# Convolution taps and gate columns in the order of the source on VectorE, and the first weight roundings behind the first chunk of h

## The chip, the cores and the metric

One core of a Trainium2 chip runs the kernel. The metric is the device time of one execution in microseconds; the time before is 794.59 us, the median of three runs (794.29 to 795.41). The engines are TensorE (PE, with its weight loads as PEld), VectorE (DVE), ScalarE (ACT), GpSimd (POOL) and SyncE (SP), whose queue issues the DMAs here.

## The reference

One decoder layer on 512 positions of 2048 channels. The part that matters, cut:

```python
c_act = silu(c)
mod = c_act @ w_ada + b_ada                      # 3 x 2048 values: shift, scale, gate
h = x * (1 + scale) + shift
q, k, v, g_attn, glu_a, glu_b, g_conv = split(h @ w_in)
y_attn = banded_sink_attention(q, k, v, rel_bias, sinks) * silu(g_attn)   # window 128, 16 q heads, 4 kv heads
u = glu_a * sigmoid(glu_b)                       # 1024 channels
u = causal_depthwise_conv(u, conv_w) + conv_b    # 31 taps
y_conv = (silu(layer_norm(u)) @ w_pw + b_pw) * silu(g_conv)
y = concat(y_attn, y_conv) @ w_out
x = layer_norm(ALPHA * x + gate * y)
```

## The kernel before

All large products run at about fp32 precision as three passes. Each fp32 operand is rounded to `hi` (fp32r) on ScalarE (L175), and `lo = raw - hi` is taken on another engine (L176, VectorE unless the call names GpSimd). `mm3` then adds hi*hi (L188), hi*lo (L189) and lo*hi (L190) into one PSUM tile. Where the weights are the left operand, L188 and L189 read `wh` and L190 reads `wl`; in the product with `w_out` the weights are on the right, so L189 reads `wl`.

Stage 1 (`ph1`, to about 200 us) builds h in 16 chunks of 128 channels. For each chunk VectorE reduces two 128 x 2048 blocks of `w_ada` with silu(c) (L225), takes `s1 = scale + 1` (L244), ScalarE makes `hh` and `h` from `xT` (L246, L247), and VectorE makes `hl` (L248). At once `fix` and `rot` project the chunks done so far to the 16 column tiles of glu_a and glu_b: `fix` keeps six PSUM tiles open, `rot` sums the other ten through SBUF (`acc`). `plan()` gives the order: h 0, fix 0, rot 3 over chunk 0, rot 4 over chunk 0, h 1, fix 1, rot 5 over two chunks, and so on. `make_u` turns a pair of column tiles into the gated input `u` of the convolution, eight tiles in all.

Stage 2 runs `project` for the column blocks of 256 in the order k, v, then q and g_attn for each of four head groups, then four blocks of g_conv (`gc`). A projection is four weight blocks of 512 KB; a block is `load_w` (raw, rounding, `wl`), then 24 matmuls into two PSUM tiles, with stages of the attention of the head group before (`between`, two per block: scores L440 to L455, transposes L462, values L472 to L484). An attention step of 128 queries takes four of these places, so two blocks. After each block `take(conv, budget)` draws work for VectorE from a generator, until the costs that it yields use up the budget. `wl` is made on GpSimd up to the second gc projection and on VectorE in the last two. Weight tiles (`wr`, `wh`, `wl`) have three buffers each. k is evicted by ScalarE and VectorE in eight pairs of instructions (L397 and L398), q in four (L503 and L504), g_attn and gc by ScalarE alone (L510, L527).

The generator `conv_and_gate` yields taps and gate columns. The convolution takes channel tiles in four pairs, and in a pair the 31 taps alternate between the two tiles, each tap an instruction on 128 x 512 that adds to a sum in PSUM (`cva`, two buffers, L294 and L300); the last tap writes `cv` in SBUF. That is 248 instructions, 240 of which yield 0.6; the opening tap of a tile yields nothing. Behind every second yielded tap comes one half of a gate column: a DMA of 512 KB of `w_ada` (`wag`, one buffer for each half) and a reduction on VectorE (L316), 32 in all at a cost of 1.4. The budgets are 4.0 for k and v, 2.3 for q, g_attn and the first two gc blocks, 4.8 for the last two gc blocks (L69). Then `take(fill, 1000)` (L625) draws what is left, and the first part of the layer norm over channels.

Stage 3 multiplies the attention half of y with `w_out`, a column block of 512 at a time into four PSUM tiles (`quad`): three of the pools `prj` or `att`, and the fourth of `cva`. It also finishes the norm; then come the pointwise product, the second half of `w_out` and the last layer norm.

The order of instructions on each engine is not that of the source. A planner (`schedule_with_timeline_sim=True`, L805) follows the program with its own durations and puts on each engine, when it falls free, the first instruction in the source's order whose inputs and buffers are ready. So a tap, which is almost always ready, can be placed ahead of an instruction that stands earlier in the source but has to wait. On the chip an engine then takes its instructions in the order that was planned.

Of the kernel before, what the change touches and what calls it, by code (L numbers as in the profile page):

```python
# [13 lines left out]
AF = mybir.ActivationFunctionType  # L14
ALU = mybir.AluOpType
# [4 lines left out]
S = 512  # L20
# [27 lines left out]
SM_CB = 48  # L48
# [8 lines left out]
N_FIXED = 3  # L57
# [44 lines left out]
def parts_of(k0, n):  # L102

    m = -(-n // 4)
    cuts = [k0 + n * a // m for a in range(m + 1)]
    return list(zip(cuts[:-1], cuts[1:]))
# [34 lines left out]
def build(tc, xT, x, c, wadaT, smalls, win, wpw, wout, relT, sinks, ln_g, ln_b, out):  # L141
    nc = tc.nc
    es = ExitStack()

    blocks, off = {}, 0
    for key, k0, n, cols in w_in_blocks():
        width = n * sum(w for _, w in cols)
# [11 lines left out]
    sm = pp.tile([P, SM_N], F32, name="sm")  # L159
# [3 lines left out]
    first = pp.tile([P, 1], F32, name="first")  # L163
# [6 lines left out]
    wp = es.enter_context(tc.tile_pool(name="wp", bufs=3, reuse_waits="tile"))  # L170
    cvp = es.enter_context(tc.tile_pool(name="cvp", bufs=10, reuse_waits="tile"))

    def split(raw, hi, lo, engine=None):

        nc.scalar.activation(hi, raw, AF.Copy)  # L175
        (engine or nc.vector).tensor_tensor(lo, raw, hi.bitcast(F32), op=ALU.subtract)  # L176

    def load_w(src, off, width, pool=None, space=1024, engine=None):
        pool = pool or wp
        raw = pool.tile([P, space], F32, name="wr")  # L180
        nc.sync.dma_start(raw[:, :width], src[off:off + P * width].rearrange("(p e) -> p e", p=P))
        hi = pool.tile([P, space], F32R, name="wh")
        lo = pool.tile([P, space], F32R, name="wl")
        split(raw[:, :width], hi[:, :width], lo[:, :width], engine)
        return hi, lo

    def mm3(ps, lh, ll, rh, rl, start, stop):
        nc.tensor.matmul(ps, lh, rh, start=start, stop=False)  # L188
        nc.tensor.matmul(ps, lh, rl, start=False, stop=False)  # L189
        nc.tensor.matmul(ps, ll, rh, start=False, stop=stop)  # L190

    def silu_c(pool, psp, tag):

        warm = psp.tile([P, S], F32, name="warm", tag=tag)
        for i in range(N_WARM):
            nc.tensor.matmul(warm[:, :P], ones, ones, start=True, stop=True)
        crow = pool.tile([P, D], F32, name="wa", bufs=WA_BUFS)[0:1, :]
        nc.sync.dma_start(crow, c)
        cb = pool.tile([P, D], F32, name="cb", bufs=1)
        parts = [slice(i * S, (i + 1) * S) for i in range(4)]  # L200

        chl = [(hh[0:1, NK - 4 + i, :], hl[0:1, NK - 4 + i, :]) for i in range(4)]
        for part, (hi, lo) in zip(parts, chl):
            split(crow[:, part], hi, lo)
        for part, (hi, lo) in zip(parts, chl):
            ps = psp.tile([P, S], F32, name="psc", tag=tag)
            nc.tensor.matmul(ps, ones_r[0:1, :], hi, start=True, stop=False)
            nc.tensor.matmul(ps, ones_r[0:1, :], lo, start=False, stop=True)
            nc.scalar.activation(cb[:, part], ps, AF.Silu)
        warm = psp.tile([P, S], F32, name="warm", tag=tag)  # L210
        for i in range(N_WARM2):
            nc.tensor.matmul(warm[:, :P], ones, cb[:, D - P:], start=True, stop=True)
        return cb
# [15 lines left out]
    glu = {}  # L229
    ph1 = ExitStack()  # L230
    p1 = ph1.enter_context(tc.tile_pool(name="p1", bufs=2))
    ps1 = ph1.enter_context(tc.tile_pool(name="ps1", bufs=2, space=PSUM))
    fixed = [ps1.tile([P, S], F32, name=f"fix{t}", bufs=1) for t in range(2 * N_FIXED)]
    cb = silu_c(p1, ps1, "rot")
# [13 lines left out]
        nc.vector.tensor_tensor(hl[:, k, :], h, hh[:, k, :].bitcast(F32), op=ALU.subtract)  # L248

    def fix(k):  # L250
        wh, wl = load_w(win, *blocks["fix", k], p1, N_FIXED * 256)
        for t in range(2 * N_FIXED):
            cs = slice(t * P, (t + 1) * P)
            mm3(fixed[t], wh[:, cs], wl[:, cs], hh[:, k, :], hl[:, k, :], k == 0, k == NK - 1)
# [6 lines left out]
    def rot(i, k0, n):  # L261
        ps = [ps1.tile([P, S], F32, name="rot") for _ in range(2)]
        for ka, kb in parts_of(k0, n):
            wh, wl = load_w(win, *blocks["rot", i, ka])
            for t in range(2):
                for k in range(ka, kb):
                    o = (k - ka) * 256 + t * P
                    mm3(ps[t], wh[:, o:o + P], wl[:, o:o + P], hh[:, k, :], hl[:, k, :], k == k0, k == k0 + n - 1)
        for t in (0, 1):
            if k0 == 0:  # L270
                nc.scalar.activation(acc[i, t], ps[t], AF.Copy)
            else:
                nc.vector.tensor_tensor(acc[i, t], ps[t], acc[i, t], op=ALU.add)  # L273
        if k0 + n == NK:
            make_u(i, acc[i, 0], acc[i, 1])

    def make_u(i, a, b):
        sig = p1.tile([P, S], F32, name="sig", bufs=1)
        nc.scalar.activation(sig, b, AF.Sigmoid)
        glu[i] = new_u()  # L280
        nc.vector.tensor_tensor(glu[i][:, PAD:], a, sig, op=ALU.mult)
# [3 lines left out]
    def conv_steps():  # L285

        sums = {}
        for i0 in range(0, NC8, 2):
            for j in range(TAPS):
                for i in (i0, i0 + 1):  # L290
                    w = sm[:, SM_CW + i * TAPS + j:SM_CW + i * TAPS + j + 1]
                    if j == 0:
                        sums[i] = ps2.tile([P, S], F32, name="cva", bufs=2)
                        nc.vector.tensor_scalar(sums[i], glu[i][:, :S], w, sm[:, SM_CB + i:SM_CB + i + 1],  # L294
                                                op0=ALU.mult, op1=ALU.add)
                        continue
                    if j == TAPS - 1:
                        cv[i] = cvp.tile([P, PAD + S], F32, name="cv", tag="u")
                    dst = cv[i][:, :S] if j == TAPS - 1 else sums[i]
                    nc.vector.scalar_tensor_tensor(dst, glu[i][:, j:j + S], w, sums[i], op0=ALU.mult, op1=ALU.add)  # L300
                    yield 0.6

    def gate_steps():

        cb = ys.tile([P, D], F32, name="cbg", tag="sgc0")
        nc.sync.dma_start(cb, c.to_broadcast([P, D]))
        nc.scalar.activation(cb, cb, AF.Silu)
        junk = cvp.tile([P, PAD + S], F32, name="junkg", tag="u")[:, :S].bitcast(BF16)
        for j in range(2 * NK, 3 * NK):
            dst = mod[:, j:j + 1]  # L310
            for half in range(2):
                hs = slice(half * S * 2, (half + 1) * S * 2)
                wa = ys.tile([P, 2 * S], F32, name="wag", tag=f"y{2 + half}")
                nc.sync.dma_start(wa, wadaT[j * P:(j + 1) * P, hs])
                first = sm[:, SM_ADA + j:SM_ADA + j + 1]
                nc.vector.tensor_tensor_reduce(junk, wa, cb[:, hs], 1.0, dst if half else first, ALU.mult, ALU.add,  # L316
                                               dst)
                yield 1.4

    def conv_and_gate():  # L320
        gate = gate_steps()
        for n, cost in enumerate(conv_steps()):
            yield cost
            if n % 2:
                yield next(gate, 0)
        yield from gate
# [42 lines left out]
    def project(c0, evac, budget, new_ps, gen=None, after=None, between=lambda: None, engine=nc.gpsimd):  # L369
        ps = [new_ps() for _ in range(2)]  # L370
        for k0 in range(0, NK, 4):
            wh, wl = load_w(win, *blocks["col", c0, k0], engine=engine)
            for t in range(2):
                between()
                for kk in range(4):
                    o = kk * 256 + t * P
                    mm3(ps[t], wh[:, o:o + P], wl[:, o:o + P], hh[:, k0 + kk, :], hl[:, k0 + kk, :],
                        k0 + kk == 0, k0 + kk == NK - 1)
            take(gen or conv, budget)
            if after:  # L380
                after(k0)
        for t in range(2):
            evac(t, ps[t])
# [21 lines left out]
    for k0 in range(0, NK, 4):  # L405
        wh, wl = load_w(win, *blocks["col", C_V, k0], engine=nc.gpsimd)
        for n in range(NB):
            o = vps[n // 2][:, n % 2, :]
            for kk in range(4):
                k = k0 + kk  # L410
# [6 lines left out]
    for n in range(NB):  # L417
        split(vps[n // 2][:, n % 2, :].rearrange("p (j d) -> p j d", j=NKV), vhl[:, n, :, 0, :], vhl[:, n, :, 1, :])
# [209 lines left out]
    def w_out_block(n, kp):  # L628
        return load_w(wout, (n * 8 + kp) * P * 1024, 1024)
# [9 lines left out]
    for n in range(4):  # L639
        cs = slice(n * S, (n + 1) * S)  # L640
        ps = quad(n)
        for kp in range(4):
            wh, wl = w_out_block(n, kp)
# [45 lines left out]
    for o in range(4):  # L689
        ps = [prj() for _ in range(2)]  # L690
        for k0 in range(0, NC8, 4):
            wh, wl = load_w(wpw, (o * 2 + k0 // 4) * P * 1024, 1024)
            for t in range(2):
                for kk in range(4):
                    w0 = kk * 256 + t * P
                    k = k0 + kk
# [3 lines left out]
        for t in range(2):  # L700
            i = 2 * o + t
            yc = small("yc")[:, :S]
            nc.vector.scalar_tensor_tensor(yc, ps[t], sm[:, SM_PB + i:SM_PB + i + 1], sgc[i // 4][:, i % 4, :],
                                           op0=ALU.add, op1=ALU.mult)
# [30 lines left out]
    for n in range(2):  # L735
        ps = quad(n)
        for kp in range(4, 8):
            wh, wl = w_out_block(n, kp)
# [8 lines left out]
    for t in range(NB):  # L747
# [12 lines left out]
        for m in range(4):  # L760
            ms = slice(m * S, (m + 1) * S)
            nc.vector.scalar_tensor_tensor(z[:, t, ms], z[:, t, ms], mv[:, t, 0:1], lg[:, ms],
                                           op0=ALU.subtract, op1=ALU.mult)
        nc.vector.reciprocal(mv[:, t, 3:4], mv[:, t, 2:3])
        for m in range(4):
            ms = slice(m * S, (m + 1) * S)
            nc.vector.scalar_tensor_tensor(z[:, t, ms], z[:, t, ms], mv[:, t, 3:4], lb[:, ms],
                                           op0=ALU.mult, op1=ALU.add)
# [40 lines left out]
```

## Time and profile before

| | |
|---|---|
| median of three runs | 794.59 us |
| profiled execution, device time | 794.61 us |
| span of its instructions | 792.8 us |
| TensorE matmuls, weight loads | 763.5, 629.0 us busy |
| VectorE | 646.4 us busy, 1053 instructions |
| ScalarE, GpSimd | 344.4, 124.9 us busy |
| mean granted clock of TensorE | 0.991 |

The profile is one execution. Times of rows count from the start of the span. Busy time of TensorE overlaps from one matmul to the next, so a busy TensorE may still be at half its clock; the granted clock says which (1.00 is 2.4 GHz, 0.5 is 1.2 GHz). An idle time in brackets stands before the row's first instruction, with what ended it.

### The profile page before, as it was taken

The page shows a single profiled execution, that of the slowest core. Times are in us where ns is not written, and L with a number is a line of the kernel's source. Part 1 is how long each engine was busy: PE and PEld are TensorE (multiplying, and loading weights), DVE is VectorE, ACT ScalarE, POOL GpSimd, SP SyncE. Part 2 cuts the span into 40 slices and gives each one's busy share as a digit, 9 for nine tenths or more (in the row PEclk, how much of TensorE's full clock was granted, in tenths as well). Part 3 has the DMA queues.
Part 4 walks back from the last instruction along what each step waited for, and adds up shares of the span by engine and source line. Part 5 has one row for each costly group of instructions (what it writes and reads, how often), then busy time and mean ns, then how long its engine had stood idle before and what let it go on. Part 6 is the DMA issues. An engine that isn't in the chain of part 4 may idle for free.

```text
span 792.8 us, 9710 instructions
## 1 busy us (share of the span) xinstructions
PE 763.5 (96%) x3522; PEld 629.0 (79%) x3522; DVE 646.4 (82%) x1053; ACT 344.4 (43%) x576; POOL 124.9 (16%) x78
## 2 busy tenths in 40 slices
PE   5999999999999889899999999999999999999994
PEld 4787888878898678688888888888888888888883
DVE  6888988946999999999999999764674219867797
ACT  4543333333342143666585668534475335433000
POOL 0000000002535253243333333000000000000000
PEclk9999999999999999999999999999999999999998
DMA  8999998513777676332222222223223233684033
GB/s 311 414 412 407 346 322 305 191 59 112 243 259 239 230 247 211 108 110 77 91 95 83 79 81 80 81 82 105 87 76 121 88 107 120 226 296 156 0 107 107
DMA packets 39091, 136.11 MB, mean 172 GB/s; under 512 B 4338, under 2 KB 6786, under 8 KB 34818
## 3 DMA queue, kind: packets, MB, share of 16 engines
q1 hardware_dynamic: 39042, 135.49, 48.9%
q8 instruction: 27, 0.44, 0.2%
q14 instruction: 22, 0.17, 0.1%
HBM read 131.26 MB, written 4.22 MB: 171 GB/s over the span
## 4 chain that ended last, share of the span: by engine, by line
PE 79%; DVE 15%; DMA 3%; issue 2%; ACT 1%; SPq 0%; DVEq 0%; ACTq 0%
PE prj L190 13%; PE prj L188 13%; PE prj L189 13%; DVE junkg L316 6%; PE rot L188 5%; DVE cva L300 4%; PE rot L189 4%; PE rot L190 4%; PE fix L188 3%; PE att L190 3%; PE att L189 3%; PE att L188 3%; PE fix L189 3%; PE fix L190 3%; DMA wag<-in_wadaT 2%
## 5 line engine op out<-in xcount | busy, mean ns | idle before, releaser
L175 ACT ACTIVATE wh<-wr 128x1024 fp32r<-128x1024 f32 (+2 forms) x129 | 127.3, 996 | 177.1 <-PE prj L189 68.0
L188 PE MATMUL prj<-hh,wh 128*128 128x512 f32 x480 | 190.5, 397 | 2.6 <-ACT sg L510 2.1
L189 PE MATMUL prj<-hl,wh 128*128 128x512 f32 x480 | 189.1, 394 | 0.0
L190 PE MATMUL prj<-hh,wl 128*128 128x512 f32 x480 | 188.1, 394 | 0.0
L176 POOL TENSOR_TENSOR wl<-wr,wh 128x1024 fp32r<-128x1024 f32 x48 | 120.0, 2503 | 316.4 <-ACT wh L175 297.6
L300 DVE SCALAR_TENSOR_TENSOR cva<-u,sm,cva 128x512 f32<-128x512 f32 x232 | 163.0, 746 | 0.6
L176 DVE TENSOR_TENSOR wl<-wr,wh 128x1024 fp32r<-128x1024 f32 (+3 forms) x81 | 89.0, 1103 | 71.4 <-ACT wh L175 71.2
L188 PEld LDWEIGHTS prj<-hh,wh 128*128 128x128 f32 x480 | 90.9, 189 | 22.9 <-ACT sg L510 2.6
L190 PEld LDWEIGHTS prj<-hh,wl 128*128 128x128 f32 x480 | 90.8, 189 | 18.7
L189 PEld LDWEIGHTS prj<-hl,wh 128*128 128x128 f32 x480 | 91.1, 190 | 18.0
L225 DVE CUSTOM_DVE_ANT_0 junk<-wa,cb,sm 128x2048 bf16<-128x2048 f32 (+1 forms) x32 | 72.9, 2278 | 2.7 <-DMA wa<-in_wadaT 2.7
L188 PE MATMUL rot<-hh,wh 128*128 128x512 f32 x160 | 62.5, 395 | 1.0 <-DVE acc L273 1.0
L189 PE MATMUL rot<-hl,wh 128*128 128x512 f32 x160 | 62.5, 390 | 0.0
L190 PE MATMUL rot<-hh,wl 128*128 128x512 f32 x160 | 62.4, 391 | 0.0
L451 ACT ACTIVATE e<-e,least 128x257 f32<-128x257 f32 (+1 forms) x64 | 30.4, 476 | 37.0 <-DVE least L446 34.4
L189 PE MATMUL fix<-hl,wh 128*128 128x512 f32 x96 | 38.8, 404 | 0.0
L190 PE MATMUL fix<-hh,wl 128*128 128x512 f32 x96 | 38.2, 398 | 0.0
L188 PEld LDWEIGHTS rot<-hh,wh 128*128 128x128 f32 x160 | 30.3, 190 | 8.9 <-DVE acc L273 1.1
L246 ACT ACTIVATE hh<-xt,mod,s 128x512 fp32r<-128x512 f32 x16 | 13.0, 815 | 51.7 <-DVE mod L225 45.3
L190 PEld LDWEIGHTS rot<-hh,wl 128*128 128x128 f32 x160 | 30.0, 188 | 6.8 <-DVE wl L176 0.3
L273 DVE TENSOR_TENSOR acc<-rot,acc 128x512 f32<-128x512 f32 x34 | 23.1, 688 | 14.9 <-PE rot L190 14.9
L189 PEld LDWEIGHTS rot<-hl,wh 128*128 128x128 f32 x160 | 30.0, 188 | 6.4
(186 smaller groups left out, 1307.4 us busy)
## 6 DMA issues: line engine op xcount, KB each, us to landing
wr<-in_win SPq DMA_DIRECT2D x68, 512.0 KB, 3.6
wa<-in_wadaT SPq DMA_DIRECT2D x30, 1024.0 KB, 7.8
wag<-in_wadaT SPq DMA_DIRECT2D x32, 512.0 KB, 4.2
wr<-in_wout SPq DMA_DIRECT2D x32, 512.0 KB, 3.3
wr<-in_win SPq DMA_DIRECT2D x24, 384.0 KB, 8.2
xt<-in_xT SPq DMA_DIRECT2D x16, 256.0 KB, 8.6
wr<-in_wpw SPq DMA_DIRECT2D x8, 512.0 KB, 3.3
xs<-in_x SPq DMA_DIRECT2D x16, 256.0 KB, 5.4
```

What stands on the lines that cost most here:

```text
L175: nc.scalar.activation(hi, raw, AF.Copy)
L176: (engine or nc.vector).tensor_tensor(lo, raw, hi.bitcast(F32), op=ALU.subtract)
L188: nc.tensor.matmul(ps, lh, rh, start=start, stop=False)
L189: nc.tensor.matmul(ps, lh, rl, start=False, stop=False)
L190: nc.tensor.matmul(ps, ll, rh, start=False, stop=stop)
L225: nc.vector.tensor_tensor_reduce(junk[:, part], w[:, part], cb[:, part], 1.0, first, ALU.mult, ALU.add, mod[:, j:j + 1])
L246: nc.scalar.activation(hh[:, k, :], xt, AF.Identity, bias=mod[:, k:k + 1], scale=s1)
L273: nc.vector.tensor_tensor(acc[i, t], ps[t], acc[i, t], op=ALU.add)
L300: nc.vector.scalar_tensor_tensor(dst, glu[i][:, j:j + S], w, sums[i], op0=ALU.mult, op1=ALU.add)
L316: nc.vector.tensor_tensor_reduce(junk, wa, cb[:, hs], 1.0, dst if half else first, ALU.mult, ALU.add, dst)
L451: nc.scalar.activation(e[:, hd, :nkeys + 1], e[:, hd, :nkeys + 1], AF.Exp, bias=least[:, hd:hd + 1], scale=-1.0, accum_out=total[:, hd:hd ...
```

## The change

`tc.keep_in_program_order(ins)` ties an instruction behind the instruction that was traced just before it on its engine: in the planned order it cannot come earlier than that one. It adds no wait on the chip. The changed kernel calls it for every tap and every reduction of a gate column on VectorE; nothing else on VectorE is tied. With `pin`, it also calls it for the rounding (L175 on ScalarE) of the weights of `fix` for chunk 0 and of the two `rot` calls over chunk 0 alone; the instruction traced before the first of these on ScalarE is the second activation of chunk 0, `h` (L247). Budgets, buffers, data and the count of instructions stay as they are.

```diff
-    def split(raw, hi, lo, engine=None):
-        nc.scalar.activation(hi, raw, AF.Copy)
+    def split(raw, hi, lo, engine=None, pin=False):
+        rounded = nc.scalar.activation(hi, raw, AF.Copy)
+        if pin:
+            tc.keep_in_program_order(rounded)
         (engine or nc.vector).tensor_tensor(lo, raw, hi.bitcast(F32), op=ALU.subtract)
...
-        wh, wl = load_w(win, *blocks["fix", k], p1, N_FIXED * 256)
+        wh, wl = load_w(win, *blocks["fix", k], p1, N_FIXED * 256, pin=k == 0)
...
-            wh, wl = load_w(win, *blocks["rot", i, ka])
+            wh, wl = load_w(win, *blocks["rot", i, ka], pin=k0 == 0 and n == 1)
...
-                        nc.vector.tensor_scalar(sums[i], glu[i][:, :S], w, sm[:, SM_CB + i:SM_CB + i + 1],
-                                                op0=ALU.mult, op1=ALU.add)
+                        tc.keep_in_program_order(
+                            nc.vector.tensor_scalar(sums[i], glu[i][:, :S], w, sm[:, SM_CB + i:SM_CB + i + 1],
+                                                    op0=ALU.mult, op1=ALU.add))
...
-                    nc.vector.scalar_tensor_tensor(dst, glu[i][:, j:j + S], w, sums[i], op0=ALU.mult, op1=ALU.add)
+                    tc.keep_in_program_order(
+                        nc.vector.scalar_tensor_tensor(dst, glu[i][:, j:j + S], w, sums[i], op0=ALU.mult, op1=ALU.add))
...
-                nc.vector.tensor_tensor_reduce(junk, wa, cb[:, hs], 1.0, dst if half else first, ALU.mult, ALU.add,
-                                               dst)
+                tc.keep_in_program_order(
+                    nc.vector.tensor_tensor_reduce(junk, wa, cb[:, hs], 1.0, dst if half else first, ALU.mult,
+                                                   ALU.add, dst))
```

## Rows read from the trace of the kernel before

**Rows 1.** The page, part 1: busy us, share of the span, instructions.

```profile
PE 763.5 (96%) x3522; PEld 629.0 (79%) x3522; DVE 646.4 (82%) x1053; ACT 344.4 (43%) x576; POOL 124.9 (16%) x78
```

**Rows 2.** Stretches: length, each engine's busy us and count, granted clock, DMA share, GB/s.

```profile
200.00:260.00 60.00, 60.00 (x357) 53.63 (x356) 58.17 (x114) 20.58 (x25) 28.08 (x14) 1.00 0.74 251
260.00:340.00 80.00, 71.77 (x317) 57.46 (x316) 79.00 (x126) 33.44 (x64) 29.90 (x14) 0.96 0.56 187
340.00:500.00 160.00, 160.00 (x785) 132.13 (x785) 158.08 (x329) 105.33 (x225) 59.32 (x36) 1.00 0.27 90
505.00:553.00 48.00, 48.00 (x221) 39.55 (x220) 27.28 (x39) 22.09 (x33) 0.00 (x0) 1.00 0.27 89
...
600.00:640.00 40.00, 40.00 (x178) 33.15 (x177) 11.61 (x12) 13.18 (x17) 0.00 (x0) 1.00 0.31 106
```

**Rows 3.** Timeline of TensorE's matmuls, 260 to 340: start, us, instruction, idle before.

```profile
272.80 0.38 PE L440 MATMUL att<-kh,qs 128*128 128x256 f32 x1 [2.98 <-DVE qs L504]
...
296.82 0.50 PE L188 MATMUL prj<-hh,wh 128*128 128x512 f32 x1 [2.14 <-ACT sg L510]
...
324.17 0.50 PE L472 MATMUL att<-pth,vhl 128*128 128x512 f32 x1 [1.33 <-DVE ptl L176]
...
329.28 0.66 PE L462 MATMUL att<-ident,e 128*128 128x128 f32 x4 [1.19 <-DVE least L446]
```

**Rows 4.** Timeline of VectorE, first and last subtraction of the first q.

```profile
272.06 0.68 DVE L504 SCALAR_TENSOR_TENSOR qs<-prj,qs 64x512 fp32r<-64x512 f32 x1
...
280.18 0.69 DVE L504 SCALAR_TENSOR_TENSOR qs<-prj,qs 64x512 fp32r<-64x512 f32 x1
```

**Rows 5.** Line L300, the taps: count, ns min/median/max, first and last start.

```profile
L300 DVE SCALAR_TENSOR_TENSOR cva<-u,sm,cva x232: 661/748/759, 201.2 to 503.1; 128x512 f32<-128x512 f32 x116
L300 DVE SCALAR_TENSOR_TENSOR cv<-u,sm,cva x8: 728/734/748, 292.2 to 505.8; 128x512 f32<-128x512 f32 x8
```

**Rows 6.** Timeline of ScalarE, second eviction of the second gc projection.

```profile
513.63 0.58 ACT L527 ACTIVATE sgc<-prj 128x512 f32<-128x512 f32 x1
```

**Rows 7.** Timeline of VectorE, five taps, first gc wl, first w_out wl.

```profile
218.50 3.38 DVE L300 SCALAR_TENSOR_TENSOR cva<-u,sm,cva 128x512 f32<-128x512 f32 x5
...
501.29 1.22 DVE L176 TENSOR_TENSOR wl<-wr,wh 128x1024 fp32r<-128x1024 f32 x1
...
549.22 1.23 DVE L176 TENSOR_TENSOR wl<-wr,wh 128x1024 fp32r<-128x1024 f32 x1 [0.26 <-ACT wh L175]
```

**Rows 8.** Line L316, the first halves of the gate columns.

```profile
L316 DVE CUSTOM_DVE_ANT_0 junkg<-wag,cbg,sm x16: 1268/1360/3337, 210.6 to 319.5; 128x1024 bf16<-128x1024 f32 x16
```

**Rows 9.** The page, part 6: issues, KB each, median us to landing.

```profile
wag<-in_wadaT SPq DMA_DIRECT2D x32, 512.0 KB, 4.2
```

**Rows 10.** Timeline of TensorE, first matmuls with w_out.

```profile
560.06 0.40 PE L189 MATMUL prj<-wl,hh 128*128 128x512 f32 x1
560.29 0.40 PE L190 MATMUL prj<-wh,hl 128*128 128x512 f32 x1
...
561.22 0.39 PE L188 MATMUL cva<-wh,hh 128*128 128x512 f32 x1
```

**Rows 11.** Groups of VectorE by line, 340 to 500: count, busy us, mean ns.

```profile
L300 DVE SCALAR_TENSOR_TENSOR cva<-u,sm,cva 128x512 f32<-128x512 f32 x147 | 103.2, 747 | 0.4
...
L453 DVE RECIPROCAL total<-total 128x4 f32<-128x4 f32 x12 | 2.0, 170 | 0.6 <-ACT e L451 0.6
```

**Rows 12.** Timeline of all engines, the first chunk.

```profile
13.50 0.15 DVE L244 TENSOR_SCALAR s<-mod 128x1 f32<-128x1 f32 x1
13.66 1.45 ACT L175 ACTIVATE wh<-wr 128x768 fp32r<-128x768 f32 x3 [5.58 <-DMA wr<-in_win]
...
15.03 0.80 ACT L246 ACTIVATE hh<-xt,mod,s 128x512 fp32r<-128x512 f32 x1
...
15.88 2.93 PE L188 MATMUL fix<-hh,wh 128*128 128x512 f32 x6 [6.51 <-ACT hh L246]
...
18.60 1.05 PE L188 MATMUL rot<-hh,wh 128*128 128x512 f32 x2
```

More of the change, by code (lines that the diff above doesn't have):

```diff
@@ L171, in build, with load_w @@
     cvp = es.enter_context(tc.tile_pool(name="cvp", bufs=10, reuse_waits="tile"))
-    def split(raw, hi, lo, engine=None):
-        nc.scalar.activation(hi, raw, AF.Copy)
+    def split(raw, hi, lo, engine=None, pin=False):
+        rounded = nc.scalar.activation(hi, raw, AF.Copy)
+        if pin:
+            tc.keep_in_program_order(rounded)
         (engine or nc.vector).tensor_tensor(lo, raw, hi.bitcast(F32), op=ALU.subtract)
-    def load_w(src, off, width, pool=None, space=1024, engine=None):
+    def load_w(src, off, width, pool=None, space=1024, engine=None, pin=False):
         pool = pool or wp
@@ L183, in load_w @@
         lo = pool.tile([P, space], F32R, name="wl")
-        split(raw[:, :width], hi[:, :width], lo[:, :width], engine)
+        split(raw[:, :width], hi[:, :width], lo[:, :width], engine, pin)
         return hi, lo
```

## The prediction

> **What bounds the kernel now.** Read the page's shares first. TensorE's matmuls are busy 763.5 of 792.8 us and VectorE 646.4 [rows 1]; an average over stages says little, so the stretches come next [rows 2]. TensorE is the bound: fully busy from 340 to 553 at a granted clock of 1.00, and idle for 80 - 71.77 = 8.2 us only between 260 and 340, where its clock is also granted at 0.96 on average, which costs another 4% of 80 us, 3.2 us. So 11.4 us lie in that stretch; the rest of what TensorE loses is the start and the tail, which this change hardly touches.
>
> VectorE is as full as TensorE from 200 to 500 (58.17 of 60, 79.00 of 80, 158.08 of 160) and then suddenly not (27.28 of 48) [rows 2]. The timeline of TensorE names the waits of 260 to 340: 2.98 us for qs, 2.14 for an eviction by ScalarE, 1.33 for ptl, 1.19 for least [rows 3]; three of the four end on VectorE. VectorE's own timeline shows why the first is long: the four qs subtractions of one projection run from 272.06 to 280.87, with taps and gate columns between them [rows 4].
>
> Last, the taps. 240 of the 248 are L300, the last starts at 505.82 [rows 5]. Where do they stand in the source? A block of K or V draws 4 tap steps and 2 gate columns, a block of q or g in the first two head groups 2 and 1 (the gate ends there, after 64 tap steps), every later block 4 tap steps, a block of the third and fourth gc projection 8. So when the third gc projection begins, right after ScalarE has evicted the second at 513.6 [rows 6], the source has drawn 64 + 6 projections x 4 blocks x 4 = 160 steps, with the 6 opening taps 166, and 82 are left. The trace had none left 8 us earlier. The planner has used taps as filler, ahead of their place; the change takes that from it.
>
> **The early stretch, 200 to 340.** A tap can no longer pass the VectorE instruction traced before it: the four kl, vhl or qs subtractions, and later the pieces of attention. These stand ahead of the next projection's taps, so the qs subtractions come in one go instead of over 8.8 us. At most this returns the whole 11.4 us. Against it: VectorE is the bound up to the first q eviction, taps run from 201.2 on [rows 5] between earlier instructions of the source, and can no longer fill gaps there (some six, an estimate, x 0.66 = 4 us; five taps in a row take 3.38, [rows 7]), and no tap may fill the wait for a gate column. A gate column takes 1.36 us at the median and 3.34 at most [rows 8]; its 512 KB land 4.2 us after issue [rows 9], and there are two buffers, so a column comes about every (4.2 + 1.4) / 2 = 2.8 us, while the source has 16 of them up to the end of V. I estimate the loss at up to 6 us. Of the range from -11.4 to +6 I take -4: the waits at 296, 324 and 329 go (2.14 + 1.33 + 1.19 = 4.7 us) with the second half of the clock loss (1.6), the wait at 272 stays and grows by 2 or so. What is late next there is the first q eviction.
>
> **The late stretch, from 505.** Now 82 taps, and 4 more of the second gc projection's last block at 505, are still to do. 86 x 0.66 = 56.8 us. VectorE's other work from 505 to 553 is 27.28 less the last tap, 26.5 us [rows 2]; this includes the wl of the eight weight blocks that start up to 549.22 [rows 7], the last of which is the first of w_out, in source order behind all taps. Sum 83.3 us, so VectorE is through at 588.3. TensorE wants that wl at 560.06 [rows 10]: 28 us late. The planner picks, on each engine, the first in source order among what is ready, and a tap is always ready (two chains alternate), so wl does not pass it. It would not help either: the fourth output tile of w_out's first column block is a cva tile [rows 10], and both cva buffers hold the last two channels' sums until their taps end.
>
> What hides it: VectorE, no longer filled up before 505, can begin the third projection's taps behind that projection's first wl, which starts at 501.29 [rows 7]. Between 340 and 500 lie 12 attention steps [rows 11] of two blocks each, so 24 blocks of 6.7 us; in source order they would bring 4 taps each, 96 x 0.66 = 63 us, beside the rest, 158.1 less 103.2 for the 147 taps of the commonest form and some 6 for eight others, 49 us [rows 2, 11]: 112 of 160, 70%. So 30% of the 11 us between wl and use, 3 us, is made good; at most all 16 taps of two blocks, 10.6 us. And TensorE can run the two of three products that use wh alone: for three output tiles and three weight buffers 3 x 3 x 2 x 2 = 36 matmuls at 0.23 us a step [rows 10], 8.3 us. That it takes products in such an order when wl is late is seen at the start, where six L188 of fix and then two of rot run before the first L189 [rows 12]. With wl in time for some, 54 matmuls, 12.4 us. Loss: 28 - 3 - 8 = 17 us; bounds 28 - 10.6 - 12.4 = 5 and, with no cover, 28. Of these I take 17, as the cover by wh is the one the trace shows. Part of it falls into the third and fourth gc projection, whose block needs 8 x 0.66 + 1.22 = 6.5 us on VectorE against 5.5 on TensorE (24 x 0.23); the sum is the same. A wait this long also costs clock: the two longest waits of 260 to 340 cost 3.2 us together [rows 2, 3], so 1.6, between 0 and 3.2.
>
> Nothing gives this back: VectorE is busy 11.61 of 40 us between 600 and 640 [rows 2], so the normalisation still ends before its users, but TensorE has no spare time to make up.
>
> **The start.** The first weights land and s1 is there within 0.01 us of each other, at 13.65: today the three roundings go first and hh starts at 15.03, 1.37 later [rows 12]. Pinned, hh starts at 13.66, h 0.70 behind it at 14.36, and the rounding of the first weights at 15.06 to 15.16 with 0.74; the first matmul needs both, so 15.9 against 15.88. hl comes 1.4 earlier, wl 1.4 later, and TensorE is then at half its rate, six matmuls in 2.93 us [rows 12], so neither is missed. +0.1 us; bounds -0.7 (one activation less ahead of the first matmul) and +2.7 (a reduction of chunk 1, with twice the columns of a gate column's 1.36 us [rows 8], gets ahead of hl in the new gap). The two later roundings stand beside TensorE's eight matmuls on the first one.
>
> **Sum.** -4 + 17 + 1.6 + 0.1 = +14.7 us on 794.61, the profiled execution's own time (span 792.8 and 1.8 around it; the median, 794.59, is the same): 809.3.
>
> **A rule against this.** The stretches show VectorE full until 500 and 57% busy behind it [rows 2]. The Trainium skill (Perfetto Trace Analysis, Identifying the Most-Contended Engine) would rank engines by occupancy over the window, and TensorE by its weight loads: 82% and 79% [rows 1], with 18% of VectorE's span free. By it, work moved within VectorE's 82% costs nothing, and the time stays 794.6; the same page's advice to look within each regime goes the other way, and the trace so far bears out the regimes.
>
> **Rivals.**
> - Faster. The freed evictions are worth their 11.4 us and VectorE's lag is hidden to its lower bound of 5 us, or to nothing. 794.6 - 11.4 + 5 = 788, or 783. For it: three of four waits end on VectorE [rows 3], and unfilled time on VectorE absorbs lateness all through 260 to 500. Against it: it needs two blocks' taps done ahead of TensorE, and no wait left at the first q eviction. It decides when fewer than about 50 taps are left at 513.
> - Gate columns block. If VectorE stands before each pinned gate column until K, V and the first q are over, 20 columns at the largest 3.34 instead of 1.5 us, it is late by some 20 x 1.8 / 3 = 12 us more where POOL and VectorE overlap a third of the time: 821. Against it: half of the columns take 1.36 us or less [rows 8], and VectorE's two idle us of 200 to 260 [rows 2] are all that gate columns can have waited there.
> - No change. Gain and loss meet, or free time on VectorE over the whole span takes the lag, as by occupancy (82%, [rows 1]). 794.6. That the pins do nothing is excluded nearly: the taps end 82 taps ahead of their place [rows 5].
>
> **How the numbers follow.** Forecast 0.62, with its own range 800 to 820; faster 0.27; gate columns 0.05; no change 0.06. Time 809. The range from 785 to 821 leaves out half of the faster case, the far end of the forecast and most of the gate case, about 0.2. Faster by over 0.2% (1.6 us, about what a measurement tells from no change): 0.27; within: 0.06; slower: 0.62 + 0.05 = 0.67.
>
> **What would show it.** In the profile after: the last tap at about 580 instead of 505.82; VectorE below 80% in 340 to 500 and nearly full from 505 to 580; TensorE idle for some 17 us between 520 and 590, ended by wl L176 or by cva, with a granted clock below 1.00 there; wl of the first w_out block late; fewer waits at 294 to 330; qs subtractions in one go; the first fix matmul within 0.3 us of 15.88. It is wrong if TensorE has no wait over 3 us behind 505, if the last tap starts before 540, or if the first q eviction is over by 273.

## The result, and the profile after

The changed kernel takes 814.62 us (median of 4 runs, 814.03 to 815.62) against 794.69 (4 runs, 794.29 to 795.41): a ratio of 1.0251, 95% interval 1.0233 to 1.0269, so 19.9 us slower. 809 was forecast, in a range of 785 to 821. The profiled execution took 815.03 us, with a span of 813.3.

The stretches first, with the columns of [rows 2]:

```profile
200.00:260.00 60.00, 60.00 (x356) 53.62 (x355) 57.78 (x107) 20.49 (x25) 27.34 (x13) 1.00 0.76 252
260.00:340.00 80.00, 75.70 (x346) 62.40 (x346) 66.14 (x116) 37.55 (x77) 31.57 (x15) 0.96 0.59 197
340.00:500.00 160.00, 159.80 (x783) 132.48 (x782) 124.04 (x268) 101.84 (x217) 57.32 (x34) 1.00 0.25 85
505.00:553.00 48.00, 48.00 (x217) 39.55 (x216) 47.82 (x70) 20.91 (x29) 0.00 (x0) 1.00 0.27 88
553.00:600.00 47.00, 25.82 (x105) 20.51 (x104) 44.91 (x67) 8.68 (x12) 0.00 (x0) 0.78 0.14 45
```

VectorE (third busy time) has moved: from 158.08 to 124.04 us in 340 to 500, from 27.28 to 47.82 in 505 to 553. TensorE (first) is busy 4 us more in 260 to 340, and then only 25.82 of 47 us from 553 on, at a mean granted clock of 0.78. Over the whole span VectorE's occupancy fell, from 82% to 80%, while the kernel lost 20 us.

TensorE's timeline shows where. The matmul that starts the product with w_out, the last one before the wait, the ones after it, and the second column sum of the norm:

```profile
554.28 0.39 PE L190 MATMUL prj<-wh,hh 128*128 128x512 f32 x1
...
566.29 0.39 PE L192 MATMUL prj<-wh,hl 128*128 128x512 f32 x1
587.87 0.79 PE L190 MATMUL cva<-wh,hh 128*128 128x512 f32 x1 [21.18 <-DVE cv L304]
588.46 0.63 PE L191 MATMUL cva<-wl,hh 128*128 128x512 f32 x1
...
606.55 1.12 PE L556 MATMUL att<-tot,ones 128*128 128x512 f32 x2 [1.89 <-DVE tot L585]
```

(L188 to L190 of before are L190 to L192 now, L300 is L304, L316 is L321, L176 is L178 in VectorE's rows, L440 is L445, L504 is L509.) One wait of 21.18 us stands in front of the first matmul into a `cva` tile. Before, that matmul ran without a wait at 561.22 [rows 10]. The releaser is a tap, the last of the first channel tile of the pair (587.07 to 587.81). Line L304 answers to [rows 5], and names who waited for it:

```profile
L304 DVE SCALAR_TENSOR_TENSOR cva<-u,sm,cva x232: 725/747/757, 206.1 to 586.4; 128x512 f32<-128x512 f32 x116
L304 DVE SCALAR_TENSOR_TENSOR cv<-u,sm,cva x8: 731/739/747, 332.1 to 587.7; 128x512 f32<-128x512 f32 x8
...
  PE cva L190: 21.2, 1
```

The last tap starts at 587.7 and not 505.8, at the same 747 ns. VectorE's own timeline over that stretch, with the first three wl of w_out:

```profile
548.83 1.22 DVE L178 TENSOR_TENSOR wl<-wr,wh 128x1024 fp32r<-128x1024 f32 x1
...
550.62 0.68 DVE L178 TENSOR_TENSOR hl<-y,hh 128x512 fp32r<-128x512 f32 x1
...
552.54 1.22 DVE L178 TENSOR_TENSOR wl<-wr,wh 128x1024 fp32r<-128x1024 f32 x1
553.68 3.38 DVE L304 SCALAR_TENSOR_TENSOR cva<-u,sm,cva 128x512 f32<-128x512 f32 x5
556.97 1.22 DVE L178 TENSOR_TENSOR wl<-wr,wh 128x1024 fp32r<-128x1024 f32 x1
558.11 29.05 DVE L304 SCALAR_TENSOR_TENSOR cva<-u,sm,cva 128x512 f32<-128x512 f32 x44
587.07 1.40 DVE L304 SCALAR_TENSOR_TENSOR cv<-u,sm,cva 128x512 f32<-128x512 f32 x2
588.39 1.28 DVE L568 TENSOR_TENSOR tot<-tot,cv 128x512 f32<-128x512 f32 x2
```

44 taps in a row and the two that close the last pair; `wl` of three weight blocks lies ahead of them. So TensorE has all three products for three of the four output tiles in three weight blocks, 54 matmuls from 554.28 to 566.52, and stops when of these three blocks only the `cva` tile is left.

The account, from the two profiled executions. Before, TensorE came to w_out like this:

```profile
558.97 1.02 PE L551 MATMUL att<-tot,ones 128*128 128x512 f32 x2
559.42 0.80 PE L188 MATMUL prj<-wh,hh 128*128 128x512 f32 x1
```

The product with w_out begins at 554.28 instead of 559.42, 5.1 us earlier. Of this, 0.4 is the norm's first column sum, which ran just ahead of it before and now runs behind the wait, at 593.77: -4.7. Wait at `cva`: 21.58 from matmul to matmul less a step of 0.23, +21.3. Nine steps at or near half rate behind it (587.87 to 591.70 in place of 9 x 0.23 = 2.1), at a granted clock of 0.50: about +1.8. A wait of TensorE for `tot`, the second column sum, which did not exist before: 2.29 less 0.23, +2.1. Sum +20.5, against spans of 813.3 - 792.8 = +20.5.

The early stretch, in the timeline of TensorE (to [rows 3]) and of VectorE (to [rows 4]):

```profile
274.93 0.58 PE L445 MATMUL att<-kh,qs 128*128 128x256 f32 x1 [4.30 <-DVE qs L509]
```

```profile
274.19 0.68 DVE L509 SCALAR_TENSOR_TENSOR qs<-prj,qs 64x512 fp32r<-64x512 f32 x1
274.90 1.28 DVE L321 CUSTOM_DVE_ANT_0 junkg<-wag,cbg,sm 128x1024 bf16<-128x1024 f32 x1
...
276.12 1.41 DVE L304 SCALAR_TENSOR_TENSOR cva<-u,sm,cva 128x512 f32<-128x512 f32 x2
277.56 1.41 DVE L509 SCALAR_TENSOR_TENSOR qs<-prj,qs 64x512 fp32r<-64x512 f32 x2
279.00 1.28 DVE L321 CUSTOM_DVE_ANT_0 junkg<-wag,cbg,mod 128x1024 bf16<-128x1024 f32 x1
...
280.32 0.69 DVE L509 SCALAR_TENSOR_TENSOR qs<-prj,qs 64x512 fp32r<-64x512 f32 x1
```

One wait is left of the four, and it has grown from 2.98 to 4.30 us. The subtractions still have taps and gate columns between them. The start:

```profile
13.90 0.81 ACT L248 ACTIVATE hh<-xt,mod,s 128x512 fp32r<-128x512 f32 x1 [5.81 <-DVE s L246]
14.62 0.80 ACT L249 ACTIVATE h<-xt,mod,s 128x512 f32<-128x512 f32 x1
15.32 1.13 ACT L175 ACTIVATE wh<-wr 128x768 fp32r<-128x768 f32 x2
...
16.20 2.92 PE L190 MATMUL fix<-hh,wh 128*128 128x512 f32 x6 [6.83 <-ACT wh L175]
...
41.87 1.43 PE L190 MATMUL fix<-hh,wh 128*128 128x512 f32 x5 [1.39 <-ACT hh L248]
```

The releaser of the first matmul is now the rounding of the weights and no longer hh, as intended; s1 itself was 0.2 us later in this execution.

### The profile page after: what moved, and what is told of

Its sections match the earlier page's. It is cut to its first block, busy times and chain, and to the rows that moved or that the text cites. A ratio compares the mean times of both kernels' runs of the same rounds, so it can differ in the third digit from the quotient of the medians.

```text
span 813.3 us, 9695 instructions
## 1 busy us (share of the span) xinstructions
PE 764.0 (94%) x3522; PEld 630.7 (78%) x3522; DVE 651.4 (80%) x1053; ACT 342.8 (42%) x576; POOL 123.0 (15%) x78
## 4 chain that ended last, share of the span: by engine, by line
PE 73%; DVE 19%; DMA 3%; issue 1%; ACT 1%; POOL 0%; SPq 0%; DVEq 0%; POOLq 0%; ACTq 0%
PE prj L192 11%; PE prj L191 11%; PE prj L190 11%; DVE cva L304 9%; PE rot L190 4%; PE rot L191 4%; PE rot L192 4%; DVE junkg L321 3%; PE fix L190 3%; PE fix L191 3%; PE att L191 3%; PE att L192 3%; PE att L190 3%; PE fix L192 3%; DMA wag<-in_wadaT 2%; DVE wl L178 2%
## 5 line engine op out<-in xcount | busy, mean ns | idle before, releaser
L175 ACT ACTIVATE wh<-wr 128x1024 fp32r<-128x1024 f32 (+3 forms) x129 | 127.1, 996 | 191.8 <-PE cva L192 55.9
L190 PE MATMUL prj<-hh,wh 128*128 128x512 f32 x480 | 189.3, 395 | 0.0
L192 PE MATMUL prj<-hh,wl 128*128 128x512 f32 x480 | 188.3, 393 | 0.0
L178 POOL TENSOR_TENSOR wl<-wr,wh 128x1024 fp32r<-128x1024 f32 x48 | 119.0, 2481 | 301.0 <-ACT wh L175 277.7
L304 DVE SCALAR_TENSOR_TENSOR cva<-u,sm,cva 128x512 f32<-128x512 f32 x232 | 160.1, 747 | 0.6
L178 DVE TENSOR_TENSOR wl<-wr,wh 128x1024 fp32r<-128x1024 f32 (+2 forms) x81 | 88.6, 1101 | 44.7 <-ACT wh L175 44.2
L190 PEld LDWEIGHTS prj<-hh,wh 128*128 128x128 f32 x480 | 90.9, 189 | 19.2 <-issue 0.4
L192 PEld LDWEIGHTS prj<-hh,wl 128*128 128x128 f32 x480 | 90.8, 189 | 19.0
L190 PE MATMUL rot<-hh,wh 128*128 128x512 f32 x160 | 62.6, 391 | 0.5 <-ACT acc L273 0.5
L192 PE MATMUL rot<-hh,wl 128*128 128x512 f32 x160 | 61.8, 390 | 0.0
L192 PE MATMUL fix<-hh,wl 128*128 128x512 f32 x96 | 36.6, 393 | 0.0
L190 PEld LDWEIGHTS rot<-hh,wh 128*128 128x128 f32 x160 | 30.2, 189 | 7.8 <-ACT acc L273 0.9
L192 PEld LDWEIGHTS rot<-hh,wl 128*128 128x128 f32 x160 | 30.0, 188 | 6.5
L190 PE MATMUL fix<-hh,wh 128*128 128x512 f32 x96 | 27.3, 413 | 8.2 <-ACT wh L175 6.8
L321 DVE CUSTOM_DVE_ANT_0 junkg<-wag,cbg,sm 128x1024 bf16<-128x1024 f32 x16 | 32.1, 2007 | 2.2 <-DMA wag<-in_wadaT 1.4
```

The costliest lines, as they stand in the source:

```text
L175: rounded = nc.scalar.activation(hi, raw, AF.Copy)
```

## Experiments

Theory A: the taps of the later channel pairs can no longer run ahead, so they still hold the two `cva` buffers when w_out's first column block wants one, and that wait is the loss. Rivals: gate columns or roundings carry it; or TensorE waits for VectorE's queue as a whole, its `wl` above all.

**One part at a time.** Each run pins one of the three kinds of instruction alone. For the roundings alone, against the changed kernel and cut (the taps of L304 lose their pin in the same way):

```diff
-                        tc.keep_in_program_order(
-                            nc.vector.tensor_scalar(sums[i], glu[i][:, :S], w, ...))
+                        nc.vector.tensor_scalar(sums[i], glu[i][:, :S], w, ...)
...
-                tc.keep_in_program_order(
-                    nc.vector.tensor_tensor_reduce(junk, wa, cb[:, hs], ...))
+                nc.vector.tensor_tensor_reduce(junk, wa, cb[:, hs], ...)
```

> Only the pins on the first weight roundings; taps and gate columns as before. Theory A (the 20 us come from late taps that hold the two cva buffers of PSUM when w_out wants one): no wait behind 505, the start 0.3 us later, 794 to 796.5 us. Rival (the rounding pins shift stage 1 and carry a part of the loss or of the 5 us by which w_out began earlier): below 792 or above 798.

Measured 795.01 us against 794.72: ratio 1.0000 (0.9988 to 1.0011). The first matmul starts at 15.92. A wait of 1.39 us that ends at 41.36 and one of 0.45 at 29.98 are there, in place of two, 0.4 and 0.6 us long, that end at 72.2 and 172.6 before. The roundings carry nothing, neither loss nor gain.

> Only the gate columns pinned; taps and roundings free. Theory A: taps still fill gaps ahead of their place and end before 515, no wait at w_out, 790 to 798 us. Rival (gate columns): taps end later than 540 and w_out waits, over 802 us.

Here the pins are left on the gate columns alone (the roundings lose theirs too). 794.47 us against 794.72: 0.9993 (0.9981 to 1.0005). The last tap ends at 507.4, and the waits of TensorE that end at 273, 297 and 325 are much as before (3.15, 2.24 and 1.86 us). Gate columns alone do nothing.

> Only the taps pinned; gate columns and roundings free. Theory A: the last tap ends at 585 to 590, TensorE waits about 21 us at the first cva tile of w_out, 812 to 816 us. Rival (pinned gate columns hold VectorE up, and the taps behind them): the last tap before 560, no wait over 5 us, 790 to 800 us.

Pins on both tap lines alone. 819.30 us against 794.72, ratio 1.0307 (1.0281 to 1.0334): outside the interval that A gave by 3 us, on the slower side; the last tap ends at 590.9. TensorE's timeline at w_out:

```profile
590.33 0.80 PE L190 MATMUL cva<-wh,hh 128*128 128x512 f32 x1 [19.57 <-DVE cv L304]
```

The taps alone make the wait. What they don't make alone is the gain before 340: there waits of 4.29, 1.95 and 2.76 us end at 272.5, 321.2 and 324.7, at a granted clock of 0.91 in 260 to 340. Neither taps nor gate columns alone freed the evictions; the changed kernel, with both (and the roundings, worth nothing alone), did.

**Which taps.** The pin is kept for one channel pair or for the other three.

```diff
-                    tc.keep_in_program_order(
+                    (tc.keep_in_program_order if i0 == 0 else id)(
                         nc.vector.scalar_tensor_tensor(dst, glu[i][:, j:j + S], w, sums[i], op0=ALU.mult, op1=ALU.add))
```

> The changed kernel with the taps of the first channel pair pinned (the 60 steps beside the gate columns) and those of the other three free; gate columns and roundings stay pinned. Theory A (what costs is that taps of the later pairs can't run ahead): no cva wait at w_out, the 5 us by which w_out began earlier stay at least in part, 789 to 795 us. Rival C (the first pair's delay is carried on to the end): a wait at w_out of over 5 us, 800 us or more.

788.72 us against 793.93: 0.9936 (0.9920 to 0.9953). No wait at `cva`; the product with w_out begins at 552.4. With `if i0 else id`, the complement:

> The complement of the run with only the first channel pair pinned: the first pair's taps are free, those of the other three pinned, gate columns and roundings as in the changed kernel. Theory A: the last tap ends at 580 to 590 and TensorE waits 15 to 22 us at w_out's first cva tile, while the waits of 290 to 330 are back: 810 to 820 us. Rival (the first pair's order decides the end of the taps as well): last tap before 560, under 800 us.

816.49 us against 794.68: 1.0269 (1.0240 to 1.0298). Two lines of TensorE:

```profile
298.98 0.80 PE L190 MATMUL prj<-hh,wh 128*128 128x512 f32 x1 [3.82 <-ACT sg L515]
...
589.74 0.80 PE L190 MATMUL cva<-wh,hh 128*128 128x512 f32 x1 [19.57 <-DVE cv L304]
```

So the early gain is the first pair's and the late loss the others'. As each run does one of them, the two halves of the forecast are shown apart. Their sum is not the whole: -5.2 and +21.8 give +16.6, and the changed kernel lost 19.9. Where TensorE waits for the last taps, it gains nothing by coming earlier; what counts is that these end at 588.5 in the changed kernel and at 590.3 here, 1.9 us later, and 21.8 - 1.9 = 19.9.

**How many taps are left.** The pins stay as changed; the source draws more taps for each weight block of the last two head groups and the first two gc projections.

```diff
-BUDGET = {"kv": 4.0, "qg": 2.3, "gc": 4.8, ...}
+BUDGET = {"kv": 4.0, "qg": 2.3, "qg2": 2.9, "gc": 4.8, ...}
...
-        project(256 * j, q_out, BUDGET["qg"], prj, between=go)
+        project(256 * j, q_out, BUDGET["qg" if j < 2 else "qg2"], prj, between=go)
...
```

The g_attn line and the first two gc projections get the same budget; in the second run `qg2` is 3.5.

> The changed kernel, but the source draws 5 taps instead of 4 for each weight block of the last two head groups and the first two gc projections: 24 taps fewer are left at the third gc projection (58 instead of 82). Theory A: the taps end 24 x 0.66 = 16 us earlier, near 573, the wait at w_out shrinks from 21 to 5 or 6 us, 797 to 801 us. Rival B (the wait is that of TensorE for VectorE's queue as a whole, whose work is the same): over 805 us.

799.54 us against 793.93, 1.0069 (1.0054 to 1.0084). The last tap ends at 573.1, and

```profile
572.52 0.79 PE L190 MATMUL cva<-wh,hh 128*128 128x512 f32 x1 [6.33 <-DVE cv L304]
```

> The same with 6 taps for each block: 34 are left at the third gc projection. Theory A: the taps end at about 557, before w_out's first cva tile is wanted, no wait there, and the 5 us gained up to 340 are kept: 788 to 792 us. Rival B: over 800 us. A third reading (VectorE is then 90% full again in 340 to 500 and evictions are late again): 793 to 797 us, with waits of TensorE before 510.

788.44 us against 793.93, 0.9930 (0.9916 to 0.9945). The last tap ends at 555.4, and the first `cva` matmul starts without a wait:

```profile
559.69 0.39 PE L190 MATMUL cva<-wh,hh 128*128 128x512 f32 x1
```

VectorE is 96% busy again between 340 and 500 (153.80 of 160 us), and yet TensorE has no wait there: the third reading falls too.

By the source's count 56 and 32 taps are left, not 58 and 34: the two opening taps of the last pair are drawn early too. The last tap ends 15.3 us earlier (588.5 to 573.1; 24 x 0.66 = 15.8 was worked out), w_out begins 0.5 earlier, and the wait shrinks by 14.9, from 21.18 to 6.33 us; the next step ends it. VectorE has 1053 instructions in all three, busy for 649 to 651 us, so the amount of its work is not what TensorE waits for: it is the place of the taps.

**Another buffer.** The direct test of the buffer decided nothing.

```diff
-        last = ps2.tile([P, S], F32, name="cva", bufs=2)
+        last = ps2.tile([P, S], F32, name="cva", bufs=2) if n else att()
```

> The changed kernel, but the fourth output tile of the first w_out column block comes from the att buffers, not from cva. Theory A (the buffer alone makes TensorE wait): the 21 us go, the next cva tile is wanted 22 us later, when the taps are all but done, 793 to 798 us. Rival B (VectorE's order: wl of the fourth and later w_out blocks stands behind the taps until 588): TensorE stops for 8 to 15 us at wl L178 between 565 and 590, 803 to 810 us.

825.87 us, 1.0393 (1.0376 to 1.0409), which neither theory gave:

```profile
589.97 2.04 PE L556 MATMUL att<-tot,ones 128*128 128x512 f32 x2 [23.83 <-DVE tot L570]
...
601.68 2.07 PE L556 MATMUL att<-tot,ones 128*128 128x512 f32 x2 [9.67 <-DVE tot L585]
```

The `cva` wait is gone, but the fourth tile was planned behind both column sums, which take `att` tiles too and stand ahead of it in the source; they need the last taps. So TensorE waited for the taps by another way, and twice. This run doesn't separate the buffer from `wl`, and no other run does; that rests on the trace after, where the three `wl` were done at 558 and a tap released the wait. No run gave `cva` a third buffer beside the eight tiles that `prj`, `att` and `cva` hold.

**The wait that is left.** The first q projection draws nothing, and the first g_attn projection its steps beside its own.

```diff
+"q0": 0, "g0": 4.6
...
-        project(256 * j, q_out, BUDGET["qg"], prj, between=go)
+        project(256 * j, q_out, BUDGET["qg" if j else "q0"], prj, between=go)
-        project(C_GA + 256 * j, g_out, BUDGET["qg"], prj, between=go)
+        project(C_GA + 256 * j, g_out, BUDGET["qg" if j else "g0"], prj, between=go)
```

On the 6-tap kernel:

> The changed kernel with 6 taps for a block of the last two head groups and the first two gc projections, and with the steps of the first q projection drawn in the first g_attn projection instead. If the remaining wait of 4.45 us at the first q eviction and the slow clock behind it come from steps that stand ahead of that eviction on VectorE: wait under 1.5 us, no slow stretch near 272, 780 to 784 us. If they come from TensorE's order (scores planned ahead of a projection) or from gate columns late from k and v: the wait stays over 3 us, 786 to 790 us.

781.05 us against 794.68: 0.9834 (0.9818 to 0.9849). On the kernel with the first pair pinned:

> Only the first channel pair's taps pinned, with the steps of the first q projection drawn in the first g_attn projection. Same question as in the run before it on a kernel with other late taps: 781 to 785 us if the steps ahead of the first q eviction are the cause, 786 to 790 us if not.

780.72 us against 794.68, 0.9830 (0.9807 to 0.9853), 0.3 us below the interval given. VectorE's timeline and the stretch there:

```profile
265.24 0.69 DVE L509 SCALAR_TENSOR_TENSOR qs<-prj,qs 64x512 fp32r<-64x512 f32 x1
266.58 0.69 DVE L509 SCALAR_TENSOR_TENSOR qs<-prj,qs 64x512 fp32r<-64x512 f32 x1 [0.66 <-ACT qs L508]
268.28 0.69 DVE L509 SCALAR_TENSOR_TENSOR qs<-prj,qs 64x512 fp32r<-64x512 f32 x1 [1.01 <-ACT qs L508]
269.63 0.69 DVE L509 SCALAR_TENSOR_TENSOR qs<-prj,qs 64x512 fp32r<-64x512 f32 x1 [0.66 <-ACT qs L508]
```

```profile
260.00:340.00 80.00, 79.68 (x376) 65.91 (x375) 70.38 (x128) 39.46 (x81) 36.35 (x16) 1.00 0.63 209
```

Now the four come in one go, waiting only for ScalarE, and TensorE is busy 79.68 of 80 us at a granted clock of 1.00. The same two budgets on the kernel before, without a pin:

> The kernel before, no pins at all, with the steps of the first q projection drawn in the first g_attn projection. If the order alone (pins) keeps early taps off the first q eviction, the planner still fills the gap with taps from later on: the waits of 269 to 330 stay within 2 us of before, 793 to 796 us. If the place of these steps in the source is what matters, pins or not: 786 to 790 us.

794.25 us against 794.13, 1.0001 (0.9990 to 1.0011), with TensorE's waits as before:

```profile
272.20 0.58 PE L440 MATMUL att<-kh,qs 128*128 128x256 f32 x1 [3.40 <-DVE qs L504]
...
297.93 0.50 PE L188 MATMUL prj<-hh,wh 128*128 128x512 f32 x1 [3.81 <-ACT sg L510]
```

Without pins the planner fills the emptied place: the four subtractions still run from 271.47 to 280.62, with taps and gate columns between them. The two kernels of 781 us beat both.

## Why the prediction was right, and where not

*The late stretch, from 505* was right in its mechanism and in the time at which VectorE is through: 588.3 was worked out, the last tap ended at 588.5. That it is so near is partly luck: from 505 on, taps kept VectorE busy for 61 us and not 56.8, and its other work for 22 and not 26.5. It had two reasons for the wait and took the wrong one as the price. It said that `wl` "does not pass" a tap that is always ready; three `wl` did pass. A pinned tap isn't always ready: it stands behind the instruction traced before it, which here is a `wl` or an `hl` of y that waits for TensorE. (The order is in the rows above; that the planner saw it so is inferred from its rule, its own times are not on record.) The second reason, `cva`, is the one that held. So the term of 17 us was mis-sized, and measured 21.3: with `wl` in time the cover was the 54 matmuls of the bound (12.4 us) and not 36 (8.3); but the 5.1 us by which TensorE came earlier were not charged against VectorE's lag, and the credit of 3 us for taps begun early hardly came. To add -4 and +17 was itself a mistake: if TensorE waits until VectorE is through, an earlier TensorE waits longer. Without the -4, the forecast's own terms give 813.3. In numbers, TensorE at the wait and VectorE through: forecast 560.06 + 8.3 = 568.4 and 588.3 - 3 = 585.3; measured 566.5 and 587.9.

*Clock*, 1.6: the steps behind the wait cost about 1.8. *A term was missing*: the norm, late with the taps, made TensorE wait 2.1 us for the second column sum. That "the normalisation still ends before its users" overlooked that this column sum is itself a user, on TensorE and in order.

*The early stretch*, -4: from the first matmul of k (197.19 before, 198.00 after) to the end of the last gc projection, TensorE took 5.5 us less. About 5 of this are waits, in the parts that were named: those at 296, 324 and 329 went, and the one at 272 grew, 2.98 to 4.30 us. The one at 296 ended on ScalarE, but ScalarE had been late from VectorE: its waits for `least` fell from 16.8 us, six waits between 250 and 345, to 7.5, three.

```profile
ACT e L451 <- DVE least L446: 16.8, 6, 5.9
```

The 1.6 us of clock did not come: before, the clock was granted at 0.5 for 3.4 us from 274.2 and for 3.4 from 298.0, after for 6.8 from 274.1, so the mean of the stretch stayed 0.96. That the subtractions come in one go was wrong; a pin holds a tap behind an eviction traced before it, but nothing holds the eviction ahead of taps traced before it, and these were late. Moving those steps ended the wait.

*The start*, +0.1: right within the 0.2 us by which s1 differed, and worth nothing in the end: 1.0000 alone. The wait of 1.39 us before 41.87 was not foreseen. The first matmul of k starts between 195.6 and 197.4 in the four profiled kernels without these pins and between 196.5 and 198.0 in the nine with them: 0.7 us later on average, within the spread and with no time lost in the run of the roundings alone.

*The rivals.* The faster one did not come true here: the changed kernel has the lag. It gave 783 to 788, and the kernels without late taps took 788.4 and 788.7, but that is luck: 788 was made of the whole 11.4 us and a lag of 5, and these kernels have half the gain and no lag. Its condition was sound, fewer than about 50 taps left at the third gc projection: with 56 left the kernel was still slower than before (799.5), with 32 faster. Gate columns blocking is refuted: 0.9993 alone, and pinned beside the taps they made the kernel faster (814.62 against 819.30 us), not slower. No change by occupancy is refuted: VectorE's share fell to 80%, and TensorE waited for it 21 us at one place.

The forecast occupancy of 70% for VectorE in 340 to 500 came out as 124.04 of 160, 78%.

## What to carry to other kernels

An instruction that fills gaps has two places: where the source draws it and where the planner puts it. To pin it is to make the source's place count, so the source's budgets have to be balanced first; with the pins and 6 taps for a block instead of 4 the same change was worth 5.5 us instead of costing 20, and the budgets of the first q and g_attn projections did nothing without pins (6 taps for a block without pins was not run). When work is moved later, ask what it still holds: here two PSUM buffers, which another engine wanted, while the amount of VectorE's work stayed the same. And when one half of a change makes TensorE come earlier, charge that to the other half.

## What the runs showed that was not expected

A gate column's reduction, 1.27 us at its shortest in every run, took 1.77 at the median and 3.51 at most for the first halves in the changed kernel, against 1.36 and 3.34 before [rows 8]; the second halves went the other way, 1.29 at the median against 1.43.

```profile
L321 DVE CUSTOM_DVE_ANT_0 junkg<-wag,cbg,sm x16: 1271/1770/3511, 208.1 to 343.6; 128x1024 bf16<-128x1024 f32 x16
L321 DVE CUSTOM_DVE_ANT_0 junkg<-wag,cbg,mod x16: 1272/1286/3182, 210.7 to 347.7; 128x1024 bf16<-128x1024 f32 x16
```

The traces tell which ones are slow: those beside a subtraction (`wl`) on GpSimd. One pair of the changed kernel:

```profile
244.40 2.40 POOL L178 TENSOR_TENSOR wl<-wr,wh 128x1024 fp32r<-128x1024 f32 x1 [3.58 <-ACT wh L175]
245.75 2.13 DVE L321 CUSTOM_DVE_ANT_0 junkg<-wag,cbg,sm 128x1024 bf16<-128x1024 f32 x1
```

The subtraction ends at 246.80 and the reduction 1.08 us later, at 247.88. Over the 13 profiled kernels it is the same: the 118 reductions that met no subtraction on GpSimd took 1.27 to 1.29 us, and each of the 198 that took over 1.3 us ended 1.07 to 1.09 us after a subtraction, as if it had done nothing until then. The taps beside such subtractions kept their 0.75 us. No run took the subtractions off GpSimd to test it.
